# Layer 0 of a two-layer inference step: queries and keys produced with features on partitions, rotated and split there, and passed through DRAM

## The chip, the cores and the metric

The kernel runs on one core of a Trainium2 chip. The metric is the device time of one execution in microseconds (us). The kernel before took 3851.68 us, the median of 3 runs (3841.71 to 3852.99).

## The reference

The reference is one inference step of a two-layer backbone on 128 context tokens (the prompt) and 1024 latent tokens on a grid 64 wide, with a model width of 1024. Layer 0 has two kinds of attention heads side by side, layer 1 retention and RWKV-7; each layer ends in a SwiGLU block. The change is in layer 0's attention:

```python
nq, nk, nv, dq, dk, dv = attn_projections(h_lat, w_in_attn[i])      # also for h_ctx
dq, dk = axial_rope(dq), axial_rope(dk)                              # latent tokens only
o_na = neighbourhood_attention(nq, nk, nv, cache_na_k, cache_na_v, na_rpb)
k_all = concatenate([dk, cache_diff_k]); v_all = concatenate([dv, cache_diff_v])
o_df = diff_attention(dq, k_all, v_all, lam, lam_init)
# axial_rope, on each half of 32 features: x1, x2 = its two quarters
#   concatenate([x1 * cos - x2 * sin, x1 * sin + x2 * cos])
# diff_attention: softmax(q0 k0) - lam * softmax(q1 k1), times v, then an RMS norm
```

There are 4 differential heads (two query and key components of 64 features, values of 128) and 8 neighbourhood heads of 64 features, which attend to a window of 8 grid rows by 16 columns and to 128 cached tokens. The context's keys and values, before any rotation, are outputs too.

## The kernel before, in words

**Numbers in two parts.** Matmuls that must be nearly exact use each fp32 operand as a high part (rounded to the type fp32r) and a low part (the rest). `split` (L71) makes them: ACT copies to the high part (L74), DVE subtracts (L75). A product is then three matmuls, high x high, high x low, low x high.

**The projection.** `attn_in` (L357) makes queries, keys and values for one of eight groups. Groups 0 to 3 are the differential heads, groups 4 to 7 are pairs of neighbourhood heads; each has three blocks of 128 weight columns. `proj_tok` (L332) loads and splits eight weight tiles of 128 x 384 and yields; then for each of 9 tiles of 128 tokens it does 8 x 3 matmuls (L350, L351, L352) whose stationary operand is the normalised input hH or hL and whose moving operand is the weights, 384 columns. The result has tokens on partitions. `sink` copies it from PSUM on ACT (L368), stores it to the DRAM tile qkv on SP's queue (L369), and for the context tile stores keys and values to the outputs. Each group has 10 steps (yields).

**Preparation of keys and queries.** At the start of a head `prep_k` (L409) loads its keys from qkv and the cache in three pieces; `stage` (L380) rotates them where the head is differential (two DVE products, L387 and L394, and a POOL addition, L397), makes the high and low parts (ACT L403 or L405, DVE L406); PE transposes them (L429) and ACT copies them to the tile K (L434, L437), which holds for each component 64 features' high parts on partitions 0 to 63 and the low parts on 64 to 127. Every unit (one query tile of 128 tokens) starts with a load of its queries from qkv (L504, or L615 and L617 for a neighbourhood tile, whose 8 rows of 16 columns are gathered), then `prep_q` (L440) does the same with three slots (high, low, high), four transposes (L446) and a DVE copy (L448) to Q.

**Units and their order.** A differential unit (`diff_unit`, L497) has scores against 9 key tiles (L518, L519), maxima on DVE (L520, L522), exponentials on ACT (L524), the difference of the two softmaxes (L541), transposes of the probabilities (`pv`, L476, with copies at L478) and the products with the values (L482). A neighbourhood unit (`na_unit`, L605) adds its mask and a bias tile nab loaded from DRAM (L624, L649). `pipe` (L567) interleaves the stages of successive units; between every two it calls `fill`, which pulls steps of other work from generators at fixed rates: in the differential stretch the projection of groups 1 to 7 (GS = 0.28 steps a place) and the modulation vectors of `ada_vec` (L165: a load aw on SP's queue and two DVE products, L181; AS = 0.3), in the neighbourhood stretch the output projection (OS = 0.34), its weights (owraw, L744), the transposed input x (L699 to L706) and the mixed tiles (`mix_k`, L750).

**Buffers and queues.** In the pipelined part the accumulator tile "mm" has one buffer; "S" has four, "T" two. Weight tiles have three raw buffers and nine of each part. The instructions are written in the order of the generators, and the compiler's tile framework then orders each engine's queue by a simulated timeline; on the chip every engine, and SP's queue of transfers, works through its own order and waits where an input is missing.

Of the kernel before, what the change touches and what calls it, by code (L numbers as in the profile page):

```python
# [11 lines left out]
F32 = mybir.dt.float32  # L12
F32R = mybir.dt.float32r
I32 = mybir.dt.int32
AF = mybir.ActivationFunctionType
ALU = mybir.AluOpType
# [25 lines left out]
SHARED = ("K", "Q", "pT", "qraw", "kraw", "st2", "st3", "mx", "sm")  # L42


class Net:
# [286 lines left out]
    def proj_tok(self, hH, hL, wsrc, ncol, pool, sink):  # L332

        nc = self.nc
        WH, WL = [], []
        for k in range(KT):
            raw = self.t(pool, [P, ncol], tag="wraw")
            nc.sync.dma_start(raw if ncol != GW else raw.rearrange("p (m c) -> p m c", c=P), wsrc(k))
            wh = self.t(pool, [P, ncol], F32R, tag="wh")
            wl = self.t(pool, [P, ncol], F32R, tag="wl")  # L340
            self.split(wh, wl, raw)
            WH.append(wh)
            WL.append(wl)
        yield
        for T in range(NT):
            pt = self.t(self.nps, [P, 512], tag="mm")
            c = slice(T * P, (T + 1) * P)
            for k in range(KT):
                mm = nc.tensor.matmul
                mm(pt[:, :ncol], lhsT=hH[k][:, c], rhs=WH[k], start=k == 0, stop=False)  # L350
                mm(pt[:, :ncol], lhsT=hH[k][:, c], rhs=WL[k], start=False, stop=False)  # L351
                mm(pt[:, :ncol], lhsT=hL[k][:, c], rhs=WH[k], start=False, stop=k == KT - 1)  # L352
            sink(T, pt)
            yield


    def attn_in(self, g, hH, hL, pool):  # L357
        nc, I, O = self.nc, self.I, self.O
        j = g if g < 4 else g - 4
        blk = 3 if g < 4 else 0  # L360
        w = I["w_in_attn"][0]

        def wsrc(k):
            return w[k * P : (k + 1) * P, :].rearrange("p (m c) -> p m c", c=512)[:, blk : blk + 3, j * P : (j + 1) * P]

        def sink(T, pt):
            st = self.t(pool, [P, GW], tag="ist")
            nc.scalar.copy(st, pt[:, :GW])  # L368
            nc.sync.dma_start(self.qkv[g][T * P : (T + 1) * P, :], st)  # L369
            if T == 0:  # L370
                if g < 4:
                    nc.scalar.dma_start(O[4][0, 0, :, j].rearrange("t c d -> t (c d)"), st[:, P : 2 * P])
                    nc.scalar.dma_start(O[5][0, 0, :, j], st[:, 2 * P :])
                else:
                    nc.scalar.dma_start(O[2][0, 0, :, 2 * j : 2 * j + 2].rearrange("t c d -> t (c d)"), st[:, P : 2 * P])
                    nc.scalar.dma_start(O[3][0, 0, :, 2 * j : 2 * j + 2].rearrange("t c d -> t (c d)"), st[:, 2 * P :])

        return self.proj_tok(hH, hL, wsrc, GW, pool, sink)

    def stage(self, p, raw, n, slots, scale, rope):  # L380

        nc = self.nc
        if rope is not None:
            cs, sn = rope
            m1 = self.t(p, [P, n, P], tag="rm1", bufs=1)
            m2 = self.t(p, [P, n, P], tag="rm2", bufs=1)
            nc.vector.tensor_tensor(  # L387
                m1.rearrange("p n (c d) -> p n c d", d=64),
                raw.rearrange("p n (c d) -> p n c d", d=64),
                cs.unsqueeze(2).to_broadcast([P, n, 2, 64]),  # L390
                op=ALU.mult,
            )
# [8 lines left out]
        if slots == 3:  # L401
            for s in (0, 2):
                nc.scalar.activation(st[:, :, s, :], rv, AF.Copy, scale=scale)  # L403
# [1861 lines left out]
```

## Time and profile before

| What | Value |
|---|---|
| median of 3 runs | 3851.68 us |
| time of the profiled execution | 3851.15 us |
| its span | 3849.4 us |
| PE busy | 3661.5 us (95%) |
| DVE, ACT, POOL busy | 2272.7, 1404.6, 1100.4 us |
| first and last projection matmul of layer 0's attention (L350) | 61.2 and 594.9 us |
| first differential scores, last neighbourhood scores | 126.9 and 878.9 us |

Busy time is the union of an engine's instructions. A line of a stretch's view gives the stretch, its length, and then each engine's busy time with the number of instructions, the mean clock granted to PE, the mean busy share of the 16 DMA engines and GB/s. A line of the groups gives the code line, the engine, what is written from what, the shape and the count; then busy us, mean ns of one, and the idle time of the engine just before them with what ended it. A line of the waits reads: who waited for whom, us in total, times, the longest. The chain of waits is followed back from the end of a stretch, at each step to what released the instruction. SPq is SP's queue of transfers.

### The profile page before, as it was taken

How to read it: one execution, taken by the hardware profiler on the slowest of the kernel's cores; microseconds unless marked ns; L12 is line 12 of the kernel's file. 1: busy time of each engine (PE TensorE's matmuls, PEld its weight loads, DVE VectorE, ACT ScalarE, POOL GpSimd, SP SyncE). 2: the span in 40 equal slices, each digit the busy share in tenths (PEclk: the TensorE clock that was granted, in tenths of full speed). 3: DMA queues.
4: the chain of work that ended last, by engine and by line, in shares of the span. 5: the costliest groups of instructions: out<-in, count | busy, mean ns of one | idle time of the engine just before them, and what ended most of it. 6: DMA issues, size and time to landing. Idle time of an engine off the chain costs nothing.

```text
span 3849.4 us, 67037 instructions
## 1 busy us (share of the span) xinstructions
PE 3661.5 (95%) x24885; PEld 3444.4 (89%) x24885; DVE 2272.7 (59%) x5106; ACT 1404.6 (36%) x3361; POOL 1100.4 (29%) x1450
## 2 busy tenths in 40 slices
PE   7999997999999999999999998999998999999998
PEld 4899996999899999999989886877777899999998
DVE  6677864665945556665244556766665774444434
ACT  3445444555333333225332333233322533334221
POOL 2000002112222224333011323665662322324430
PEclk9999997999999999999999998999999999999999
DMA  6433325542223334442334336232223212223321
GB/s 209 125 94 107 113 69 133 133 109 61 64 85 108 91 99 143 149 137 86 106 105 130 115 129 212 58 88 65 65 60 108 62 60 75 75 73 107 116 88 61
DMA packets 425399, 392.16 MB, mean 102 GB/s; under 512 B 68172, under 2 KB 370376, under 8 KB 423536
## 3 DMA queue, kind: packets, MB, share of 16 engines
q1 hardware_dynamic: 406640, 376.29, 32.3%
q10 hardware_dynamic: 13152, 7.27, 0.7%
q0 software_dynamic: 5280, 4.31, 0.6%
q8 instruction: 197, 3.23, 0.3%
q14 instruction: 130, 1.06, 0.1%
HBM read 289.32 MB, written 98.33 MB: 101 GB/s over the span
## 4 chain that ended last, share of the span: by engine, by line
PE 74%; DVE 8%; DMA 8%; POOL 3%; issue 2%; ACT 2%; SPq 0%; DVEq 0%; ACTq 0%; POOLq 0%
PE mm L82 8%; PE mm L84 8%; PE mm L83 8%; PE A L1726 3%; PE A L1724 3%; PE A L1725 3%; PE o L482 3%; DMA aw<-in_w_ada_dram 2%; PE E L1724 2%; PE E L1725 2%; PE mm L350 2%; PE E L1726 2%; PE mm L352 2%; PE mm L351 2%; DVE aacc L181 2%
## 5 line engine op out<-in xcount | busy, mean ns | idle before, releaser
L729 DVE SCALAR_TENSOR_TENSOR x<-mm,mod,x 128x128 f32<-128x128 f32 (+1 forms) x576 | 277.2, 512 | 238.7 <-PE mm L84 237.9
L1636 POOL TENSOR_TENSOR wl<-raw,wh 128x512 fp32r<-128x512 f32 x120 | 167.1, 1392 | 567.2 <-ACT wh L1635 541.3
L1635 ACT CAST wh<-raw 128x512 fp32r<-128x512 f32 x288 | 178.3, 620 | 306.4 <-PE A L1725 107.4
L181 DVE SCALAR_TENSOR_TENSOR aacc<-aw,v,aacc 128x512 f32<-128x512 f32 x280 | 228.7, 849 | 75.2 <-DMA aw<-in_w_ada_dram 74.7
L350 PE MATMUL mm<-wh,hH 128*128 128x384 f32 x576 | 200.8, 349 | 11.5 <-ACT wh L74 4.7
L352 PE MATMUL mm<-wh,hL 128*128 128x384 f32 x576 | 195.8, 341 | 4.6 <-DVE hL L261 4.6
L351 PE MATMUL mm<-wl,hH 128*128 128x384 f32 x576 | 197.3, 342 | 1.0 <-DVE wl L75 0.9
L82 PE MATMUL mm<-hH,wh 128*128 128x384 f32 x528 | 184.6, 351 | 2.6 <-ACT wh L74 2.6
L84 PE MATMUL mm<-hH,wl 128*128 128x384 f32 x528 | 180.3, 344 | 3.4 <-DVE rst L867 2.1
L83 PE MATMUL mm<-hL,wh 128*128 128x384 f32 x528 | 180.3, 342 | 0.0
L1636 DVE TENSOR_TENSOR wl<-raw,wh 128x512 fp32r<-128x512 f32 x168 | 118.8, 708 | 102.1 <-ACT wh L1635 98.3
L397 POOL TENSOR_TENSOR rm<-rm,rm 128x128 f32<-128x128 f32 (+1 forms) x40 | 27.0, 676 | 461.2 <-DVE rm L387 329.0
L75 DVE TENSOR_TENSOR wl<-wraw,wh 128x256 fp32r<-128x256 f32 (+1 forms) x184 | 90.1, 508 | 108.3 <-ACT wh L74 78.7
L1150 PE MATMUL A<-AR,BK 64*128 64x256 f32 x576 | 116.8, 418 | 31.3 <-DVE KK L1154 18.6
L524 ACT ACTIVATE P<-S,mx 128x384 f32<-128x384 f32 (+1 forms) x200 | 112.2, 570 | 88.8 <-DVE mx L522 86.6
L82 PE MATMUL mm<-mh,owh 128*128 128x384 f32 x384 | 138.5, 375 | 5.2 <-ACT owh L74 2.7
L83 PE MATMUL mm<-ml,owh 128*128 128x384 f32 x384 | 132.5, 345 | 0.0
L84 PE MATMUL mm<-mh,owl 128*128 128x384 f32 x384 | 131.3, 342 | 1.2 <-DVE owl L75 1.2
L350 PEld LDWEIGHTS mm<-wh,hH 128*128 128x128 f32 x576 | 110.2, 191 | 16.2 <-ACT ist L368 7.7
L817 PE MATMUL mm<-wh,hH 128*128 128x256 f32 x432 | 124.0, 290 | 0.0
L1150 PEld LDWEIGHTS A<-AR,BK 64*128 64x128 f32 x576 | 75.4, 194 | 53.1 <-issue 20.0
L818 PE MATMUL mm<-wl,hH 128*128 128x256 f32 x432 | 122.4, 285 | 0.0
(540 smaller groups left out, 12501.5 us busy)
## 6 DMA issues: line engine op xcount, KB each, us to landing
raw<-in_w_ffn_in_dram SPq DMA_DIRECT2D x176, 256.0 KB
aw<-in_w_ada_dram SPq DMA_DIRECT2D x160, 256.0 KB
raw<-hdr SPq DMA_DIRECT2D x132, 192.0 KB
hdr<-c SPq DMA_DIRECT2D x160, 144.0 KB
raw<-in_w_ffn_out_dram SPq DMA_DIRECT2D x88, 256.0 KB
F<-stg SPq DMA_DIRECT2D x34, 640.0 KB
stg<-st SPq DMA_DIRECT2D x12, 1536.0 KB
qkv<-ist SPq DMA_DIRECT2D x72, 192.0 KB
```

The costliest lines, as they stand in the source:

```text
L82: mm(out, lhsT=wh, rhs=xh, start=first, stop=False)
L83: mm(out, lhsT=wh, rhs=xl, start=False, stop=False)
L84: mm(out, lhsT=wl, rhs=xh, start=False, stop=last)
L181: nc.vector.scalar_tensor_tensor(acc[:, c, :], w[:, 0, :], s, acc[:, c, :], op0=ALU.mult, op1=ALU.add)
L350: mm(pt[:, :ncol], lhsT=hH[k][:, c], rhs=WH[k], start=k == 0, stop=False)
L351: mm(pt[:, :ncol], lhsT=hH[k][:, c], rhs=WL[k], start=False, stop=False)
L352: mm(pt[:, :ncol], lhsT=hL[k][:, c], rhs=WH[k], start=False, stop=k == KT - 1)
L729: self.nc.vector.scalar_tensor_tensor(x[f][:, c], pt[:, a:b], self.mod[l][jg][:, f, cd : cd + 1], x[f][:, c], op0=ALU.mult, op1=ALU.add)
L1636: eng.tensor_tensor(wl, w, wh, op=ALU.subtract)
L1724: mm(o, lhsT=wh[:, ks], rhs=xh, start=new and k == 0, stop=False, skip_group_check=True)
L1725: mm(o, lhsT=wh[:, ks], rhs=xl, start=False, stop=False, skip_group_check=True)
L1726: mm(o, lhsT=wl[:, ks], rhs=xh, start=False, stop=k == 3, skip_group_check=True)
```

## The change

The projection's operands change places. Weights are stationary and 384 tokens are moving, so a block comes out as 128 features by 384 tokens, nine (block, token group) tiles a group: keys first, then queries, then values. For the differential heads the weight columns are permuted while they are split (two pieces each), so that the two halves of every rotation pair lie 64 partitions apart; ACT copies the tile and its swapped halves from PSUM, DVE does two products with tables now laid out by feature, and the sum. ACT then writes the high part and DVE, one step later, the low part, and SP stores both to DRAM (qf). For the neighbourhood queries the parts are written in the order of the units' gathered tiles. Values are copied, transposed on PE, copied and stored token by token (vt). The context's output keys are transposed likewise. A head then loads K with two transfers and Q in three pieces of 384 tokens with four transfers each, every row of queries to both halves of the partitions; only the cached keys are split and transposed there (two transposes). These loads run in seven steps, the first six while the head before is in its last three units. The score matmuls use (high, high) and (low, low) queries against K's (high, low). A group has 19 steps, and GS becomes 0.53. The mixed tiles mh and ml have three buffers and a fourth from a later pool.

```diff
+        for m, scale in ((1, None if g < 4 else -0.125), (0, 0.125 if g < 4 else None), (2, None)):
+            ms = slice(m * P, (m + 1) * P)
+            for tg in range(TG):
+                for step in later:
+                    step()
+                later = []
+                sl = slice(tg * GW, (tg + 1) * GW)
+                pt = self.t(self.nps, [P, 512], tag="mm")
+                for k in range(KT):
+                    self.mm3(pt[:, :GW], WH[k][:, ms], WL[k][:, ms], hH[k][:, sl], hL[k][:, sl], k == 0, k == KT - 1)
+                if m == 2:
+                    st = self.t(pool, [P, GW], tag="ist")
+                    nc.scalar.copy(st, pt[:, :GW])
+                    yield
+                    o = turn(st, 3)
+                    dst = self.vt[g][sl, :]
+                    nc.sync.dma_start(dst.rearrange("(n p) c -> p n c", p=P), o.rearrange("p (n c) -> p n c", c=P))
...
+                if g < 4 or m == 1 and tg == 0:
+                    n = GW if g < 4 else P
+                    x = self.t(pool, [P, GW], tag="fx")
+                    nc.scalar.copy(x[:, :n], pt[:, :n])
                 if g < 4:
...
+                    for s in range(2):
+                        nc.scalar.copy(sw[64 * s : 64 * s + 64, a:], pt[64 - 64 * s : 128 - 64 * s, a:GW])
+                    ts = slice(tg * GW + a - P, (tg + 1) * GW - P)
+                    nc.vector.tensor_tensor(sw[:, a:], sw[:, a:], self.sin[:, ts], op=ALU.mult)
+                    nc.vector.tensor_tensor(x[:, a:], x[:, a:], self.cos[:, ts], op=ALU.mult)
+                    nc.vector.tensor_tensor(x[:, a:], x[:, a:], sw[:, a:], op=ALU.add)
+                    yield
+                if m == 1 and tg == 0:
+                    nc.sync.dma_start(ok, turn(x, 1))
+                if g >= 4:
+                    x = pt[:, :GW]
+                for u, v in self.patches(g, m, tg):
+                    nc.scalar.activation(v(hi), u(x), AF.Copy, scale=scale or 1.0)
+                if g >= 4:
+                    yield
+
+                def rest(g=g, m=m, tg=tg, x=x, hl=hl, scale=scale):
+                    hi, lo = hl[:, 0, :], hl[:, 1, :]
+                    for u, v in self.patches(g, m, tg):
+                        if scale is None:
+                            nc.vector.tensor_tensor(v(lo), u(x), v(hi), op=ALU.subtract)
+                        else:
+                            nc.vector.scalar_tensor_tensor(v(lo), u(x), scale, v(hi), op0=ALU.mult, op1=ALU.subtract)
+                    self.store_hl(g, m, tg, hl)
+
+                if g < 4:
+                    later.append(rest)
                 else:
...
+                    rest()
+                yield
...
+    def store_hl(self, g, m, tg, hl):
         nc = self.nc
...
+        dst, a, hl = self.qf[g][m], tg * GW, hl.bitcast(F32)
+        if g < 4:
+            for s in range(2):
+                for i in range(2):
+                    o = dap(dst, (i * P + 32 * s) * TOK + a, [[64 * TOK, 2], [TOK, 32], [1, GW]])
+                    nc.sync.dma_start(o, hl[64 * s : 64 * s + 64, i, :])
+            return
...
+        K = head["K"] = self.t(p, [P, 2, 10 * P], F32R, tag="K")
+        for c in range(2):
+            nc.sync.dma_start(K[:, c, :TOK].bitcast(F32), dap(self.qf[g][1], 64 * c * TOK, [[P * TOK, 2], [TOK, 64], [1, TOK]]))
...
+        def queries(tg):
+            Q = head["Q", tg] = self.t(p, [P, 2, 2, GW], F32R, tag="Q")
+            for c in range(2):
+                for i in range(2):
+                    src = dap(self.qf[g][0], (i * P + 64 * c) * TOK + tg * GW, [[0, 2], [TOK, 64], [1, GW]])
+                    nc.sync.dma_start(Q[:, c, i, :].bitcast(F32), src)
...
+    def heads_hook(self, j, T, heads, gen):
+
+        self.heads_upto(j, 7 if T >= 2 else 6, heads, gen)
+        if T >= 6 and j < 7:
+            self.heads_upto(j + 1, (2, 4, 6)[T - 6], heads, gen)
...
-        GS, AS, OS = 0.28, 0.3, 0.34
+        GS, AS, OS = 0.53, 0.3, 0.34
...
-        bp = _Bufs(both.enter_context(self.pool("kAB")), {"K": 2, "Q": 3, "pT": 2, "qraw": 2, "kraw": 2})
+        bp = _Bufs(both.enter_context(self.pool("kAB")), {"K": 2, "Q": 3, "pT": 2})
...
+            for _ in range(12):
+                next(first)
+            self.heads_upto(0, 5, head, lambda j, h: self.diff_prep(j, h, dp, ps))
+            fin(first)
```

More of the change, by code (lines that the diff above doesn't have):

```diff
@@ L39, in dap @@
     return bass.AP(tensor=ap.tensor, offset=ap.offset + offset, ap=dims)
[L42 removed]
+SHARED = ("K", "Q", "pT", "kraw", "st", "mx", "sm")
 class Net:
@@ new lines, in attn_in @@
+        WH, WL = [], []
+        for k in range(KT):
+            raw = self.t(pool, [P, GW], tag="wraw")
+            src = w[k * P : (k + 1) * P, :].rearrange("p (m c) -> p m c", c=512)[:, blk : blk + 3, j * P : (j + 1) * P]
+            nc.sync.dma_start(raw.rearrange("p (m c) -> p m c", c=P), src)
+            wh = self.t(pool, [P, GW], F32R, tag="wh")
+            wl = self.t(pool, [P, GW], F32R, tag="wl")
+            for a in zip(dense(wh), dense(wl), apart(raw)):
+                self.split(*a)
+            WH.append(wh)
+            WL.append(wl)
@@ L443, in prep_q @@
         pt = self.t(ps, [P, 512], tag="T")
         for c in range(2):
-            for s in range(2):
-                nc.tensor.transpose(pt[:, (c * 2 + s) * P : (c * 2 + s + 1) * P], st[:, c, s * 64 : s * 64 + P], self.ident)
-        Q = self.t(p, [P, 4, P], F32R, tag="Q")
-        nc.vector.tensor_copy(Q.rearrange("p a b -> p (a b)"), pt)
-        return Q
+            nc.tensor.transpose(pt[:, c * P : (c + 1) * P], st[:, c].rearrange("p b c -> p (b c)").bitcast(F32), self.ident)
+        nc.scalar.copy(K[:, :, 9 * P :], pt[:, : 2 * P].rearrange("p (c t) -> p c t", c=2))
@@ new lines, in heads_steps, with heads_upto @@
+        yield
+        queries(1)
+        yield
+        if values is not None:
+            values()
+        yield
+        queries(2)
+        yield
+    def heads_upto(self, j, k, heads, gen):
+        if j not in heads:
+            heads[j] = {"n": 0}
+            heads[j]["gen"] = gen(j, heads[j])
+        while heads[j]["n"] < k:
+            heads[j]["n"] += 1
+            next(heads[j]["gen"], None)
+    def heads_hook(self, j, T, heads, gen):
+        self.heads_upto(j, 7 if T >= 2 else 6, heads, gen)
+        if T >= 6 and j < 7:
+            self.heads_upto(j + 1, (2, 4, 6)[T - 6], heads, gen)
@@ L1943, in run @@
             self.setup(top)
-            self.qkv = [self.dram.tile([TOK, GW], F32, name=f"qkv{g}") for g in range(8)]
+            self.qf = [[self.dram.tile([2, P, TOK], F32, name=f"qf{g}{m}") for m in range(2)] for g in range(8)]
+            self.vt = [self.dram.tile([TOK, P], F32, name=f"vt{g}") for g in range(8)]
             self.odr = [self.dram.tile([TOK, P], F32, name=f"odr{g}") for g in range(8)]
@@ L1979, in attn @@
         wpool = self.wpool
+        done = set()
         def group(g):
-            return self.attn_in(g, hH, hL, wpool)
+            yield from self.first if g == 0 else self.attn_in(g, hH, hL, wpool)
+            done.add(g)
         due = {}
```

278 lines of the change are left out of this document (122 added, 156 removed).

## The prediction

> **What bounds the kernel now.** I read the page's engine totals first, then the busy time by stretch, then the chain of waits inside the stretches that the change touches, then single groups.
>
> ```profile
> PE 3661.5 (95%) x24885; PEld 3444.4 (89%) x24885; DVE 2272.7 (59%) x5106; ACT 1404.6 (36%) x3361; POOL 1100.4 (29%) x1450
> ```
>
> ```profile
> core 0: us, PE busy (x) PEld busy (x) DVE busy (x) ACT busy (x) POOL busy (x), PEclk, DMA share, GB/s
> 60.00:130.00 70.00, 60.49 (x341) 58.59 (x342) 41.40 (x88) 22.11 (x51) 12.21 (x12) 0.95 0.44 127
> 130.00:600.00 470.00, 457.27 (x2965) 445.12 (x2965) 352.07 (x875) 222.49 (x716) 23.39 (x36) 0.99 0.32 96
> 600.00:660.00 60.00, 33.69 (x171) 28.67 (x170) 27.02 (x72) 24.69 (x67) 21.95 (x32) 0.72 0.70 158
> 660.00:890.00 230.00, 222.31 (x1627) 217.17 (x1627) 138.10 (x410) 125.99 (x320) 21.47 (x32) 0.95 0.44 116
> ```
>
> Only 60 to 890 us is touched. The eight projections and the differential heads fill 60 to 600, the neighbourhood heads 640 to 890. PE is busy 457.27 of 470 us in the first long stretch and 222.31 of 230 in the last, so work taken from PE there should shorten the kernel. DVE is next, 352.07 of 470. The stretch 600 to 660 is different: 33.69 us of PE work, a clock of 0.72, and DMA at 0.70. The chain inside 130 to 600 is mostly PE, with a share that PE work does not explain:
>
> ```profile
> by line: PE mm L350 13.8%; PE mm L352 13.5%; PE mm L351 13.5%; PE o L482 9.7%; PE S L518 5.4%; PE S L519 5.2%; DVE aacc L181 5.1%; PE T L476 5.0%; DMA aw<-in_w_ada_dram 4.6%; DMA wraw<-in_w_in_attn_dram 3.5%; issue 2.6%; PE T L446 2.5%; DVE
> ```
>
> The modulation vector (aacc on DVE and its load aw) and the projection weights (wraw) hold 5.1 + 4.6 + 3.5 = 13.2% of it.
>
> **PE: transposes out, fewer transposes in.** The projection's matmul count is unchanged: before, 9 token tiles x 8 x 3 with 384 columns in each group; after, 9 tiles (three blocks, three token groups) x 8 x 3 with 384 tokens. The score matmuls are also the same in number and width. What goes is the transposition of queries (L446) and keys (L429).
>
> ```profile
> L446 PE MATMUL T<-ident,st 128*128 128x128 f32 x288 | 46.8, 288 | 1.7 <-ACT K L437 1.7
> L429 PE MATMUL T<-ident,st 128*128 128x128 f32 x160 | 24.5, 296 | 8.5 <-DVE st L406 8.5
> ```
>
> ```profile
> 304.76 0.60 PE L446 MATMUL T<-ident,st 128*128 128x128 f32 x4
> 305.11 0.42 PE L350 MATMUL mm<-wh,hH 128*128 128x384 f32 x1
> 305.37 0.33 PE L351 MATMUL mm<-wl,hH 128*128 128x384 f32 x1
> 305.54 0.34 PE L352 MATMUL mm<-wh,hL 128*128 128x384 f32 x1
> ```
>
> The 288 ns of one transpose overlap the next; the pace is read from starts. Four transposes begin at 304.76 and the matmul after them at 305.11 (0.35 us), and that matmul takes 0.26 us to its successor where the following one takes 0.17, so a batch of four costs 0.35 + 0.09 = 0.44 us, 0.11 each. Out: 288 + 160 = 448 x 0.11 = 49.3 us. In: the values now come with features on partitions and must be turned back, 9 x 8 = 72 transposes; the context's output keys, 8; the cached keys, 2 x 8 = 16. That is 96 x 0.11 = 10.6 us. Net 38.7 us off PE: half of the removed ones (24.6) lie in the neighbourhood stretch, which gains nearly all of that, while most of the added lie before 600, where 14 to 15 us remain. The other end for this price is the groups' busy time, (46.8 + 24.5)/448 = 0.159 us each, or 56 us net. I take 0.11, because 97% busy PE shows little else between the batches. The filling rate changes with the step count, 252 places x 0.28 for 70 steps to 252 x 0.53 for 133, so projections still end with the last differential unit. The first group's projection keeps its start, set by the normalised input; the larger tables of cosines, the values loaded one step later and the three instead of four buffers of the mixed tiles (the fourth in a late pool) I cost at nothing: their data are used microseconds of PE work after they arrive, and without that cover each would cost one DMA wait, such as the 9.56 or the 10.76 us in the chain below.
>
> The idle time in these two rows, 8.5 + 1.7 = 10.2 us, goes too. Part of it is the start of the neighbourhood stretch:
>
> ```profile
> 623.14 1.92 PE L429 MATMUL T<-ident,st 128*128 128x128 f32 x8 [1.47 <-DVE st L406]
> 626.79 1.12 PE L446 MATMUL T<-ident,st 128*128 128x128 f32 x4 [1.73 <-ACT K L437]
> 631.33 1.97 PE L429 MATMUL T<-ident,st 128*128 128x128 f32 x8 [3.42 <-DVE st L406]
> 634.84 1.12 PE L636 MATMUL S<-K,Q 128*128 128x128 f32 x4 [1.54 <-DVE Q L448]
> ```
>
> ```profile
> 628.74 9.56 DMA kraw<-in_cache_na_k_dram
> ...
> 649.02 10.76 DMA xr<-in_x_sample_dram
> ```
>
> From 623 to 635 PE does nothing but prepare the first neighbourhood head, with 1.47 + 1.73 + 3.42 + 1.54 = 8.2 us of idle. The change loads that head's keys and first queries during the last differential units, so this chain is gone. What is late next is on the same list: the loads of x (10.76 us) behind a DMA share of 0.70, which do not move. I book 5 of the 8.2 us here (bounds 0 and 8.2) and 10.2 - 6.6 = 3.6 us, say 4, elsewhere.
>
> **DVE, ACT, POOL.** The rows are one line of code each by stretch: L448, L406, L387 and L394.
>
> ```profile
> 60.00:600.00 540.00, 24.77 (x36) 0.98 0.34 100
> 600.00:890.00 290.00, 24.73 (x36) 0.90 0.49 125
> ```
>
> ```profile
> 60.00:600.00 540.00, 18.11 (x50) 0.98 0.34 100
> 600.00:890.00 290.00, 16.64 (x46) 0.90 0.49 125
> ```
>
> ```profile
> 60.00:600.00 540.00, 14.78 (x40) 0.98 0.34 100
> ```
>
> ```profile
> 60.00:600.00 540.00, 14.68 (x40) 0.98 0.34 100
> ```
>
> ```profile
> L75 DVE TENSOR_TENSOR wl<-wraw,wh 128x384 fp32r<-128x384 f32 x57 | 32.7, 588 | 13.2 <-ACT wh L74 12.9
> L368 ACT COPY ist<-mm 128x384 f32<-128x384 f32 x72 | 34.6, 481 | 82.1 <-PE mm L352 74.4 <-issue 4.2 <-DMA rpbd<-rpbn 1.3
> L524 ACT ACTIVATE P<-S,mx 128x384 f32<-128x384 f32 (+1 forms) x200 | 112.2, 570 | 88.8 <-DVE mx L522 86.6 <-DMA out_dram<-ist 2.2
> L524 ACT ACTIVATION_READ_ACCUMULATOR P<-S,mx 128x1 f32 x200 | 40.1, 200 | 0.0
> ```
>
> Before 600, DVE loses 24.77 + 18.11 + 14.78 + 14.68 = 72.3 us. It gains three rotations for each of 24 tiles and one subtraction for each of 48, 120 operations of 128x384 at L75's 588 ns = 70.6 us. So DVE stays as it is there, and after 600 it sheds 24.73 + 16.64 = 41.4 us. ACT loses at least L368's 34.6 us and gains some 168 operations at L368's 481 ns (four for each of 24 rotated tiles, one for 24 others, three for the 24 value tiles or their halves taken as two) = 81 us; at most 46 us more on 222.49 of 470 does not bound. POOL loses its additions and gains nothing. Free by cover, then, but through one thing: the projection's accumulator tile "mm" has a single buffer in the pipelined part. It is freed today by one copy. After the change it is read by three ACT copies for rotated tiles, and by ACT and then DVE for the neighbourhood tiles. Today's price of that hold is:
>
> ```profile
> PEld mm L350 <- ACT ist L368: 7.7, 10, 2.0
> PE mm L350 <- ACT ist L368: 4.6, 6, 1.7
> PEld mm L350 <- ACT wh L74: 6.0, 4, 3.5
> PE mm L350 <- ACT wh L74: 4.7, 3, 3.2
> ```
>
> 7.7 + 4.6 = 12.3 us over 72 tiles, 0.17 each. Twice that extra for 24 tiles and once extra for 24: 8.2 + 4.1 = 12.3 us lost. The lower bound is zero, if other work stands between; the upper bound is the slower rival below. Weights of the three later rotated groups are split in two pieces each, and the way from the last projection step of a group to the next group's first is shorter in steps; of the 10.7 us that PE waits for weights I add 3 (0 to 10.7).
>
> **DMA and SP.** The prepared parts go out and come back.
>
> ```profile
> q1 hardware_dynamic: 104432, 83.28, 34.8%
> ```
>
> ```profile
> qkv<-ist SPq DMA_DIRECT2D x72, 192.0 KB
> ```
>
> ```profile
> qraw<-qkv SPq DMA_DIRECT2D x72, 64.0 KB
> kraw<-qkv SPq DMA_DIRECT2D x16, 256.0 KB
> ```
>
> Two thirds of 72 x 192 KB (9.2 MB) of writes become twice that, as high and low parts. Reads of 4.6 + 4.1 MB become 16 key loads of 576 KB and 96 query loads of 192 KB, 27.6 MB, since each query row is loaded twice. That is about 28 MB more. Between 60 and 900 us this queue took 34.8% of 840 us for 83.28 MB, 3.5 us a MB, so 98 us of all engines over 830 us: the share rises by 12 points from 0.32 and 0.44, and stays hidden. On SP, 168 issues (72 stores, 72 + 24 loads) become 292 (148 stores of parts, 24 of values, 8 of output keys, 16 + 96 loads), 124 more; what queues behind a store that waits for its low part are the loads aw and wraw, whose waits are on the chain above. I book nothing for it, and carry it as the third case.
>
> The neighbourhood queries are stored in runs of 128 to 384 bytes, 4096 a group; at this queue's mean, 0.348 x 840 x 16/104432 = 45 ns a packet, four groups take 46 us of all engines. The Trainium skill, DMA: Bandwidth & Descriptors (Specifications), says that below 512 bytes the engine reads, modifies and writes, so these would cost more. If that doubled them, an estimate, it would be 92 us of share, still under the 0.32 that is left to fill; no run so far shows it.
>
> **Sum.** -38.7 - 5 - 4 + 12.3 + 3 = -32.4 us against the profiled execution's own 3851.15: 3818.8, and against the median of 3851.68 shown, half a us more. Forecast 3819.
>
> **The rivals.** Larger gain: the transposes carried their busy price (56 us), the idle goes whole (12 us) and the single buffer costs nothing: 3851 - 68 = 3783. For it: the idle rows above, and 0.72 of clock from 600 to 660. The Trainium skill, TensorE: Matmul & The Clock Gate (Part 1: The HAM clock gate), says idle stretches throttle the array; full clock there would give another 33.69 x 0.28 = 9 us, an estimate. Against it: PE is 97% busy, which leaves little idle to win.
>
> No change: the stretch to 600 is paced by the 13.2% of loads and modulation, now with more traffic on their queue, and passes on nothing; the neighbourhood stretch passes half of its 24. That gives -12 - 9 + 12 + 3 = -6: 3845. Against it: PE's 97%.
>
> Slower: the hold of the one accumulator buffer. Units run from the first row's 126.9 to 606.9 us:
>
> ```profile
> L518 PE MATMUL S<-K,Q x200: 273/338/690, 126.9 to 606.9; 128*128 128x384 f32 x96, 128*128 128x128 f32 x4
> ```
>
> ```profile
> ACT P L524 <- DVE mx L522: 86.6, 45, 5.1
> ```
>
> 480 us/36 = 13.3 us each, seven filling places, so a tile every 2/0.53 x 1.9 = 7.2 us. 24 matmuls at 0.17 take 4.2, which leaves 3.0 us. Three copies take 1.44; three exponentials ahead of them on ACT, (0.57 + 0.20) x 3 = 2.3; and the wait of one of them for DVE's maximum 86.6/45 = 1.9. Together 5.65 us exceeds 3.0 by 2.65, times 24 tiles 64 us, on a sum of -47.7 + 3 without that term: +19, 3870. It decides once the hold passes 3.0 us. The ACT order behind the change decides it, and this trace cannot show that.
>
> **Numbers.** The forecast has 0.50 (its own range 3795 to 3840), the larger gain 0.18, no change 0.15, slower 0.17. Leaving out most of the slower case and the far end of the gain, the range is 3776 to 3856. A measurement of this kernel tells about 0.3%, 11.6 us: faster 0.49 + 0.18 + 0.05 = 0.72, same 0.12, slower 0.16.
>
> **What would show it.** L446's and L429's transposes gone, 96 others in their place; DVE in 130 to 600 near 350 us still; PE's waits for the accumulator's readers near 25 us (over 60 means the slower case); scores of the first neighbourhood head within 3 us of the last differential product; the long stretch shorter by about 10 us, the neighbourhood one by about 20. The forecast is wrong if PE falls clearly under 95% busy before 600.

## The result: 494 us slower, and the profile after

The changed kernel takes 4343.4 us (median of 4 runs, 4338.25 to 4356.9) against 3849.3 us (4 runs) for the kernel before: a ratio of 1.1288, 95% interval [1.1263, 1.1313]. The forecast of 3819 us was wrong in sign. The profiled execution has a span of 4344.8 us, where the kernel before has 3849.4.

The engine totals of the page come first, as they did for the kernel before.

```profile
PE 3737.4 (86%) x24533; PEld 3506.1 (81%) x24533; DVE 2232.2 (51%) x5030; ACT 1395.1 (32%) x3329; POOL 1069.6 (25%) x1410
```

The 352 instructions that should leave PE have left (24885 to 24533), and DVE, ACT and POOL are a little less busy than before. No engine has become the bound; the kernel waits. The busy time by stretch of the changed kernel shows where.

```profile
core 0: us, PE busy (x) PEld busy (x) DVE busy (x) ACT busy (x) POOL busy (x), PEclk, DMA share, GB/s
60.00:130.00 70.00, 42.89 (x201) 40.91 (x201) 37.99 (x78) 17.01 (x38) 9.50 (x8) 0.81 0.22 69
130.00:600.00 470.00, 259.40 (x1385) 243.23 (x1385) 176.54 (x446) 131.67 (x419) 0.00 (x0) 0.75 0.24 79
600.00:940.00 340.00, 267.33 (x1613) 257.63 (x1612) 177.90 (x445) 119.56 (x382) 0.00 (x0) 0.87 0.33 98
940.00:1350.00 410.00, 247.79 (x1445) 239.21 (x1444) 119.56 (x375) 108.88 (x258) 43.15 (x64) 0.71 0.37 106
```

In the 470 us from 130 on PE is busy for 259.40, where it was busy for 457.27, and DVE, ACT and the DMA share (0.24 for 0.32) are all lower than before. When no engine is near full and the mean of the 16 DMA engines is low as well, the limit is one that no mean shows. The score matmuls give the stages' ends (groups on the tile K; the columns after the colon are min/median/max ns, first and last start in us):

```profile
L588 PE MATMUL S<-K,Q x200: 222/346/690, 164.0 to 937.1; 128*128 128x384 f32 x95, 128*128 128x128 f32 x5
L702 PE MATMUL S<-K,Q x16: 220/276/328, 939.7 to 1302.3; 128*128 128x128 f32 x16
L713 PE MATMUL S<-K,Q x128: 220/275/419, 989.8 to 1349.5; 128*128 128x128 f32 x128
```

By these, the first scores are 37 us later (164.0 for 126.9), the differential stretch is 293 us longer (773 for 480), the neighbourhood scores 166 us (410 for 244), and what follows them 25 us; only the gap between the two kinds of head has shrunk, from 28 us to 2.6. Among the longest waits of DVE, ACT and PE for transfers, between 60 and 1330 us of the changed kernel, are these:

```profile
DVE aacc L181 <- DMA aw<-in_w_ada_dram: 94.7, 20, 24.6
ACT ist L364 <- DMA vt<-ist: 83.8, 6, 31.2
ACT wh L74 <- DMA wraw<-in_w_in_attn_dram: 67.0, 21, 14.5
ACT hl L400 <- DMA qf<-hl: 65.0, 14, 27.0
PE S L588 <- DMA Q<-qf: 26.9, 2, 23.8
```

All are transfers of SP's queue: a modulation weight, a store of values that has to leave its buffer, a projection weight, a store of parts, a load of queries. And that queue's own line shows what it is doing (timeline of SP: start, us, line, what, how many):

```profile
121.73 4.62 SPq L471 DMA_DIRECT2D K<-qf  x2
126.39 22.33 SPq L448 DMA_DIRECT2D qf<-hl  x4
148.77 31.04 SPq L481 DMA_DIRECT2D Q<-qf  x8
179.91 10.65 SPq L448 DMA_DIRECT2D qf<-hl  x4
190.60 3.38 SPq L384 DMA_DIRECT2D vt<-ist  x2
```

In these 72 us SP issues 20 transfers. Eight query loads of 192 KB hold it for 31.04 us: 1.57 MB in 31.04 us is 51 GB/s. The stretch in the middle of these loads, where nearly nothing else moves, is this:

```profile
155.00:175.00 20.00, 3.32 (x8) 1.93 (x8) 0.45 (x2) 0.46 (x2) 0.00 (x0) 0.50 0.13 50
```

A share of 0.13 of 16 engines is 2.1 engines, and in the trace's packets exactly two are under way in 87% of these 20 us, never more than three. The transfers run on two DMA engines, while PE works 3.32 of 20 us. In the diff three kinds of transfer have a 2 as the first, slowest dimension of their DRAM side: the differential stores `[[64*TOK, 2], [TOK, 32], [1, GW]]`, the key loads `[[P*TOK, 2], [TOK, 64], [1, TOK]]` and the query loads `[[0, 2], [TOK, 64], [1, GW]]`. That is 96 x 96 KB, 16 x 576 KB and 96 x 192 KB, together 37.7 MB, which at 51 GB/s keep a pair of engines busy for 740 us.

The Trainium skill, DMA: Bandwidth & Descriptors (Why a DMA increments its semaphore by 16 and not by 1), states it: a transfer goes to the largest number of engines, at most 16, that divides the slowest dimension (other than 1) of each of its two access patterns. For these three kinds that is 2, and the share of 0.13 agrees. The prediction overlooked this rule.

So theory A is that the shape of these three patterns makes the loss, and its first rival is that the 28 MB of added traffic do, whatever its shape. Other rivals were the short runs of the neighbourhood queries' stores, the hold of the one accumulator buffer, and the order of loads behind stores.

### The profile page after: what moved, and what is told of

It reads as the page before. It is cut to its first block, busy times and chain, and to the rows that moved or that the text cites. A ratio compares the mean times of both kernels' runs of the same rounds, so it can differ in the third digit from the quotient of the medians.

```text
span 4344.8 us, 66247 instructions
## 1 busy us (share of the span) xinstructions
PE 3737.4 (86%) x24533; PEld 3506.1 (81%) x24533; DVE 2232.2 (51%) x5030; ACT 1395.1 (32%) x3329; POOL 1069.6 (25%) x1410
## 2 busy tenths in 40 slices
DMA packets 445331, 420.67 MB, mean 97 GB/s; under 512 B 82732, under 2 KB 388008, under 8 KB 443472
## 4 chain that ended last, share of the span: by engine, by line
PE 60%; DMA 11%; DVE 6%; POOL 3%; issue 2%; ACT 1%; SPq 1%; DVEq 0%; ACTq 0%; POOLq 0%
PE mm L82 8%; PE mm L84 8%; PE mm L83 8%; PE A L1792 3%; PE A L1790 3%; PE A L1791 3%; DMA aw<-in_w_ada_dram 2%; PE E L1790 2%; PE E L1791 2%; PE E L1792 2%; PE o L554 2%; DMA F<-stg 1%; DMA owraw<-in_w_out_attn_dram 1%; DMA xr<-odr 1%; PE mm L883 1%
## 5 line engine op out<-in xcount | busy, mean ns | idle before, releaser
L82 PE MATMUL mm<-hH,wh 128*128 128x384 f32 x1104 | 399.4, 363 | 88.4 <-ACT hl L400 46.9
L83 PE MATMUL mm<-hL,wh 128*128 128x384 f32 x1104 | 388.1, 352 | 8.8 <-DVE hL L261 8.8
L84 PE MATMUL mm<-hH,wl 128*128 128x384 f32 x1104 | 387.4, 352 | 3.2 <-DVE rst L933 2.4
L82 PEld LDWEIGHTS mm<-hH,wh 128*128 128x128 f32 x1104 | 220.2, 200 | 105.5 <-ACT hl L400 50.8
L83 PEld LDWEIGHTS mm<-hL,wh 128*128 128x128 f32 x1104 | 219.9, 199 | 12.3 <-DVE hL L261 9.4
L84 PEld LDWEIGHTS mm<-hH,wl 128*128 128x128 f32 x1104 | 218.6, 198 | 8.2 <-issue 2.9
L75 DVE TENSOR_TENSOR wl<-wraw,wh 128x256 fp32r<-128x256 f32 (+2 forms) x216 | 91.4, 447 | 198.1 <-ACT wh L74 169.2
L554 PE MATMUL o<-V,pT 128*128 128x128 f32 x584 | 90.1, 299 | 60.5 <-DVE mx L592 33.9
L590 DVE TENSOR_REDUCE mx<-S 128x1 f32<-128x384 f32 (+1 forms) x200 | 101.5, 540 | 68.3 <-PE S L589 68.1
L554 PEld LDWEIGHTS o<-V,pT 128*128 128x128 f32 x584 | 84.2, 211 | 64.1 <-ACT pT L550 27.1
```

Source lines behind the costliest of these rows:

```text
L82: mm(out, lhsT=wh, rhs=xh, start=first, stop=False)
L83: mm(out, lhsT=wh, rhs=xl, start=False, stop=False)
L84: mm(out, lhsT=wl, rhs=xh, start=False, stop=last)
L554: nc.tensor.matmul(o, lhsT=pT[:, i * P : (i + 1) * P], rhs=vs(b + i), start=b + i == 0, stop=b + i == nk - 1)
```

## The experiments

**wide_all** keeps number, bytes and contents of the transfers and puts the dimension of 32 or 64 rows first.

```diff
-                for i in range(2):
-                    o = dap(dst, (i * P + 32 * s) * TOK + a, [[64 * TOK, 2], [TOK, 32], [1, GW]])
-                    nc.sync.dma_start(o, hl[64 * s : 64 * s + 64, i, :])
+                for c in range(2):
+                    o = dap(dst, (64 * c + 32 * s) * TOK + a, [[TOK, 32], [P * TOK, 2], [1, GW]])
+                    nc.sync.dma_start(o, hl[64 * s + 32 * c : 64 * s + 32 * c + 32, :, :])
...
-        for c in range(2):
-            nc.sync.dma_start(K[:, c, :TOK].bitcast(F32), dap(self.qf[g][1], 64 * c * TOK, [[P * TOK, 2], [TOK, 64], [1, TOK]]))
+        for i in range(2):
+            nc.sync.dma_start(K[64 * i : 64 * i + 64, :, :TOK].bitcast(F32), dap(self.qf[g][1], i * P * TOK, [[TOK, 64], [64 * TOK, 2], [1, TOK]]))
...
-                for i in range(2):
-                    src = dap(self.qf[g][0], (i * P + 64 * c) * TOK + tg * GW, [[0, 2], [TOK, 64], [1, GW]])
-                    nc.sync.dma_start(Q[:, c, i, :].bitcast(F32), src)
+                for d in range(2):
+                    src = dap(self.qf[g][0], 64 * c * TOK + tg * GW, [[TOK, 64], [P * TOK, 2], [1, GW]])
+                    nc.sync.dma_start(Q[64 * d : 64 * d + 64, c, :, :].bitcast(F32), src)
```

> All three new kinds of transfer (stores of parts for the differential heads, key loads, query loads) are cut the other way: the dimension of 32 or 64 rows comes first and the dimension of 2 behind it. Number of transfers, bytes and runs of 1536 or 4608 bytes are the same. Theory A (a transfer whose first dimension is 2 is carried by two of the 16 DMA engines, and those two are the bound; eight query loads of 192 KB took 31 us in the changed kernel, 51 GB/s, and 37.7 MB go that way, 744 us): the loss goes, 3790 to 3870 us. Theory B (the single accumulator buffer is held too long by its three readers): nothing changes, 4330 to 4360. Theory C (the way through DRAM and SP's queue with its 124 more issues is the cost, whatever their shape): nothing changes, 4330 to 4360.

Measured: 3893.14 us (4 runs), 1.0102 [1.0064, 1.0139] of the kernel before. Of the 494 us, 450 are gone by the shape alone. The time is 23 us above the range of theory A; theories B and C, by which nothing changes, are out as the cause of the loss. The issues of query loads (L481) and of modulation weights (L128) on SP, first in the changed kernel and then in wide_all (min/median/max ns):

```profile
L481 SPq DMA_DIRECT2D Q<-qf x96: 486/1446/5928, 148.8 to 1301.4; - x96
L128 SPq DMA_DIRECT2D aw<-in_w_ada_dram x59: 327/340/12132, 62.8 to 867.7; - x59
```

```profile
L481 SPq DMA_DIRECT2D Q<-qf x96: 573/602/1252, 112.4 to 859.0; - x96
L128 SPq DMA_DIRECT2D aw<-in_w_ada_dram x59: 327/334/1640, 63.8 to 566.4; - x59
```

The median query load occupied SP for 1446 ns and now takes 602; and a weight load, whose own pattern was not touched, could take 12132 ns and now takes 1640 at most. The two-engine transfers held up everything behind them on the queue. The stretches of wide_all show PE back at work, with a DMA share that is twice the changed kernel's 0.24:

```profile
126.00:640.00 514.00, 475.94 (x2955) 457.18 (x2955) 350.43 (x883) 248.56 (x789) 0.00 (x0) 0.97 0.50 132
640.00:910.00 270.00, 223.64 (x1457) 216.64 (x1458) 119.34 (x372) 108.86 (x257) 43.15 (x64) 0.84 0.68 158
```

**wide_q** and **wide_k_st** recut only the query loads, and only the key loads and stores.

> Only the query loads are cut the other way; key loads and stores keep a first dimension of 2. Theory A: 18.9 of 37.7 MB are left on the pair, 372 us of its time, spread over some 800 us and partly hidden: 3850 to 4050 us. Theories B and C: 4330 to 4360.

> The mirror image: key loads and stores are cut the other way, query loads keep a first dimension of 2. Theory A: again 18.9 MB are left on the pair, so about the same as with only the query loads recut, 3850 to 4050 us; the sum of the two gains is larger than the whole loss if the pair is a bound that saturates. Theories B and C: 4330 to 4360.

Measured: 4097.87 us, 1.063 [1.0608, 1.0652], and 4139.63 us, 1.0739 [1.0711, 1.0767] (2 runs each). The query loads' shape is worth 245 us and that of the other two 204, together 449 where both at once give 450. Each half is 18.9 MB, so 11 to 13 us a MB. Both times lie above the range of theory A, 3850 to 4050: less of the pair's time was hidden than it supposed. The expectation held it possible that the two gains together would exceed the whole; they do not.

**old_traffic** and **old_narrow** give the kernel before (without the change) the added traffic: each tile of the projection is stored a second time, and each unit copies a tile of 192 KB within DRAM, 28 MB more in all. They differ in the DRAM patterns alone: 128 rows in the first, 2 x 64 rows in the second.

```diff
             nc.sync.dma_start(self.qkv[g][T * P : (T + 1) * P, :], st)
+            nc.sync.dma_start(self.qkv2[g][T * P : (T + 1) * P, :GW], st)
...
             nc.sync.dma_start(raw[:, 0, :], self.qkv[j][T * P : (T + 1) * P, 0:P])
+            nc.sync.dma_start(self.qkv2[j][T * P : (T + 1) * P, GW:], self.qkv2[j][T * P : (T + 1) * P, :GW])
```

In old_narrow the added lines are these:

```diff
+            nc.sync.dma_start(dap(self.qkv2[g], T * 64 * 2 * GW, [[HT * 2 * GW, 2], [2 * GW, 64], [1, GW]]), st)
...
+            two = [[HT * 2 * GW, 2], [2 * GW, 64], [1, GW]]
+            nc.sync.dma_start(dap(self.qkv2[j], T * 64 * 2 * GW + GW, two), dap(self.qkv2[j], T * 64 * 2 * GW, two))
```

> The kernel before, with about the traffic that the change adds and nothing of its work: every projection tile is stored a second time (72 x 192 KB), and every unit copies one such tile from DRAM to DRAM (72 x 192 KB) that nobody reads; 28 MB, in rows of 1536 bytes with a first dimension of 128. Theory A2 (traffic on all 16 engines delays the loads that set the pace): 3865 to 3890. If the traffic stays hidden, as the forecast had it: 3848 to 3858.

> The kernel before with the same 28 MB of extra traffic as in the earlier run on it (72 stores and 72 DRAM copies of 192 KB, read by nobody), but the DRAM side of each is cut 2 x 64 rows instead of 128 rows, the halves in two places. Theory A (a first dimension of 2 puts a transfer on two of the 16 engines): 28.3 MB at 51 GB/s are 555 us of the pair, in a stretch of 830 us; at the 11 to 13 us a MB that the two half recut kernels showed, 300 to 370 us slower, and at least 100 if much of it hides since nobody reads the data. If the loss was due to something else in the changed kernel that the recut changed too: 3860 to 3866, as with the wide rows.

Measured: 3862.6 us, 1.0032 [1.0019, 1.0044], and 4223.12 us, 1.096 [1.0923, 1.0996]. The same bytes cost 12 us in one shape, between the two ranges that were expected, and 372 in the other, where theory A had 300 to 370. The stretch 130 to 600 in old_traffic, then in old_narrow:

```profile
130.00:600.00 470.00, 451.92 (x2890) 438.82 (x2889) 347.58 (x863) 218.09 (x701) 24.30 (x37) 0.97 0.47 144
```

```profile
130.00:600.00 470.00, 295.65 (x1637) 282.98 (x1638) 195.41 (x474) 124.23 (x391) 16.11 (x22) 0.78 0.29 92
```

The second line has the look of the changed kernel: PE at 295.65 of 470, a clock of 0.78, and a DMA share that is lower, not higher, than in the first. In the packets of this stretch exactly two are under way in 48% of the time, in old_traffic in 2%. Theory A holds in both directions, and the rival of the mere traffic is left with some 12 us.

**old_twice** measures the price of the transposes: in the kernel before, each unit's four query transposes are done twice, 288 more.

```diff
-        for c in range(2):
+        for c in (0, 1, 0, 1):
             for s in range(2):
                 nc.tensor.transpose(pt[:, (c * 2 + s) * P : (c * 2 + s + 1) * P], st[:, c, s * 64 : s * 64 + P], self.ident)
```

> The kernel before, with the four transposes of every unit's queries done twice into the same place: 288 more transposes, nothing else. If a transpose on PE costs its 0.11 us on the path, as the forecast had it: 32 us more, 3875 to 3890. If PE has room for them (the forecast's gain was never there to be had): 3848 to 3860.

Measured: 3863.99 us, 1.004 [1.0023, 1.0058]. 1.004 is 15 us (9 to 22) over 288, 0.053 us each, half of the 0.11 that the prediction read from starts. The time lies between the two ranges. In the profiled execution the work from the first differential to the last neighbourhood scores is 19 us longer (771.2 for 752.0), which agrees. If a removed transpose is worth what an added one costs, the 352 net transposes that the change removes are worth 19 us, an estimate, not 38.7.

The remaining runs ask why wide_all, with fewer transposes, is still 1% slower than the kernel before.

**pool_dup**: wide_all with each query load done once, and GpSimd copying it to the other 64 partitions.

```diff
-                for d in range(2):
...
-                    nc.sync.dma_start(Q[64 * d : 64 * d + 64, c, :, :].bitcast(F32), src)
+                nc.sync.dma_start(Q[0:64, c, :, :].bitcast(F32), src)
+                nc.gpsimd.tensor_copy(Q[64:P, c, :, :], Q[0:64, c, :, :])
```

> On the kernel with all transfers recut (3893 us): each query piece is loaded once, to partitions 0 to 63, and GpSimd, which is idle in this stretch, copies it to partitions 64 to 127. 48 query transfers fewer, 9.4 MB less, 48 GpSimd copies of 64x768 more. Theory A2 (what is left of the loss is the larger traffic: the DMA share of 0.5 before 600 us and 0.8 after 650): 3855 to 3880. Theory B2 (what is left is the hold of the single accumulator buffer and the ACT and DVE order behind it): 3885 to 3900. Theory D (the rest is the first group, whose feature tiles wait for the whole normalised input): 3885 to 3900.

Measured: 3864.84 us (9 runs), 1.0047 [1.0033, 1.0061]. By the ratios, about half of wide_all's excess came from loading each query twice, in traffic and in 48 issues together, as theory A2 had it.

**first_tg**: wide_all with group 0's token groups in the order 1, 2, 0 and the first head's loads one step later, to let its first loads stand ahead.

```diff
-            for tg in range(TG):
+            for tg in (1, 2, 0) if g == 0 else range(TG):
...
-            for _ in range(12):
+            for _ in range(13):
```

> On the kernel with all transfers recut (3893 us): only for the first group the three token groups are taken in the order 1, 2, 0 (and the key loads start one step later), because the input's first token group is normalised last; the first group took 63.8 to 122.3 us where it took 61.2 to 108.6 before. Theory D: 3875 to 3885. Theories A2 and B2: 3885 to 3900.

Measured: 3884.44 us, 1.0086 [1.0067, 1.0106], inside wide_all's interval and on the border of the two ranges: no gain that can be told.

**turns**: wide_all with the accumulator taken from the tags mm, S and T in turn through the differential stretch, so that no tile waits for the readers of the one before.

```diff
             fin(first)
-            self.nps = ps
```

> On the kernel with all transfers recut (3893 us): the projection's accumulator takes the tags mm, S and T in turn for the whole differential stretch instead of the single buffer mm. Theory B2: the waits of PE for the accumulator's readers go, 3865 to 3885, unless scores and transposes lack the buffers. Theories A2 and D: 3885 to 3900.

Measured: 3930.51 us, 1.0201 [1.0181, 1.0221], slower than wide_all by 37 us and outside both ranges. The projection's tiles then come out of the buffers of the scores and the transposes: in the differential stretch PE's waits for the accumulator's readers fall from some 11 us to some 2, but the scores wait 20.8 us for ACT's exponentials where wide_all has 4.5. So this run alone does not price the hold.

**plainq**: wide_all with the neighbourhood queries' parts stored in token order, whole rows instead of runs of 128 to 384 bytes. It leaves out their reordering for the units' gathered tiles.

```diff
-        if g < 4 or m == 1:
+        if True:
...
-        if m == 1:
+        if True:
             nc.sync.dma_start(dap(dst, a, [[TOK, P], [P * TOK, 2], [1, GW]]), hl)
```

> On the kernel with all transfers recut (3893 us): the neighbourhood queries are written and stored in token order like the keys, one transfer a tile instead of two to four, no run under 1536 bytes; the reordering of the queries for the units' gathered tiles is left out, all else is done. If the 16,384 runs of 128 to 384 bytes cost something (a part of theory A2): 3870 to 3885. Theories B2 and D: 3885 to 3900.

Measured: 3877.41 us, 1.0071 [1.0051, 1.0091], about 12 us less than wide_all by the ratios, with intervals that overlap, so not clear of the noise.

**pool_first** joins wide_all, pool_dup and first_tg; **pool_plain_first** adds plainq's edit.

> All transfers recut, queries loaded once and copied by GpSimd, first group in the order 1, 2, 0: the sum of the two gains, 3865 - 8 = 3857 us if they add up; 3865 if the first group's order is worth nothing.

> The same with the neighbourhood queries written and stored in token order, so that their reordering is left out: 3857 - 16 = 3841 us if the three gains add up, which would be just under the kernel before; 3857 if the short runs cost only where the traffic is high.

Measured: 3866.91 us, 1.0035 [1.0017, 1.0053], and 3865.89 us, 1.0034 [1.0019, 1.0049]. The gains do not add up: the first group's order is worth nothing that can be told on top of pool_dup, and pool_plain_first is 9 us above the higher of its two values. With the queries loaded once, the short runs cost nothing that can be told.

**pool_swap**: pool_first with the swapped halves copied by GpSimd from SBUF, so that one ACT copy frees the accumulator of a differential tile.

```diff
-                        nc.scalar.copy(sw[64 * s : 64 * s + 64, a:], pt[64 - 64 * s : 128 - 64 * s, a:GW])
+                        nc.gpsimd.tensor_copy(sw[64 * s : 64 * s + 64, a:], x[64 - 64 * s : 128 - 64 * s, a:GW])
```

> The best of the recut kernels so far (queries loaded once, first group in the order 1, 2, 0; ratio 1.0035), with the two swapped halves of a rotated tile copied by GpSimd from the copy in SBUF instead of by ACT from the accumulator: the accumulator is free after one ACT copy instead of three, and ACT has 48 copies less before 600 us. If the hold of the accumulator and ACT's queue are what is left of the loss (theory B2), the ratio falls by 0.002 to 0.004, to about that of the kernel before. If not, it stays at 1.003 to 1.005.

Measured: 3867.24 us, 1.0035 [1.0017, 1.0053], the same as pool_first. In its differential stretch PE's waits for the accumulator's readers fall from some 12 us to some 5, while the waits of the scores for ACT's exponentials rise from 4.0 us to 9.5. Freeing the accumulator earlier gives nothing of the rest back.

**no_dep** and **no_store**, both on pool_first: every head loads group 0's keys and queries, so that no load waits for a recent store; and, in the second, groups 1 to 7 do not store their parts either.

```diff
-            nc.sync.dma_start(K[64 * i : 64 * i + 64, :, :TOK].bitcast(F32), dap(self.qf[g][1], i * P * TOK, [[TOK, 64], [64 * TOK, 2], [1, TOK]]))
+            nc.sync.dma_start(K[64 * i : 64 * i + 64, :, :TOK].bitcast(F32), dap(self.qf[0][1], i * P * TOK, [[TOK, 64], [64 * TOK, 2], [1, TOK]]))
...
-                src = dap(self.qf[g][0], 64 * c * TOK + tg * GW, [[TOK, 64], [P * TOK, 2], [1, GW]])
+                src = dap(self.qf[0][0], 64 * c * TOK + tg * GW, [[TOK, 64], [P * TOK, 2], [1, GW]])
```

In no_store also:

```diff
-                    self.store_hl(g, m, tg, hl)
+                    if g == 0:
+                        self.store_hl(g, m, tg, hl)
```

> All transfers recut, queries loaded once, first group in the order 1, 2, 0 (ratio 1.0035); all heads load the keys and queries of group 0, so that no load waits for a store of its own group; those of the other groups are stored and not used. Leaves out the use of seven groups' queries and keys. If the way out and back through DRAM (loads that wait for stores, with SP's queue behind them) is what is left: ratio 0.993 to 1.000. If not: 1.002 to 1.005.

> The same, and groups 1 to 7 do not store their parts at all (16.5 MB and some 120 transfers less): work left out. If the rest of the loss is the stores' traffic and SP's time for them: ratio 0.993 to 0.999, near the forecast's 0.992. If it is in the engines' order (ACT, DVE and PE waits of the new projection): 1.000 to 1.004.

Measured: 3874.42 us, 1.0057 [1.0037, 1.0076], and 3875.57 us, 1.0079 [1.0054, 1.0104]: both are a little above their upper ranges, neither is faster than pool_first, and why no_store is slower is not shown. Its long stretch has the DMA share of the kernel before, 0.32, and PE is still idle for 29.5 of 495 us, as in pool_dup (28.7):

```profile
130.00:625.00 495.00, 465.49 (x2882) 449.47 (x2883) 345.43 (x857) 238.67 (x755) 26.22 (x28) 0.96 0.32 86
```

So neither the wait of loads for stores nor the stores themselves are what is left. One reservation holds for all these small differences: an edit also changes the order in which the framework puts each engine's queue, and these runs do not separate the two.

## Why the prediction was wrong, step by step

**The step that failed** is the paragraph on DMA and SP: "98 us of all engines over 830 us: the share rises by 12 points from 0.32 and 0.44, and stays hidden", and "I book nothing for it". The bytes were right (392.16 MB before, 420.67 after, by the pages), but the price of a byte was taken from transfers that use 16 engines and given to patterns that use two. 37.7 MB then take 740 us of the same pair, not a few points of everything. The share of 0.32 "left to fill" was the wrong test: it fell to 0.24 while the kernel lost 494 us. The prediction did see who stands behind on SP's queue (aw and wraw, and aw leads the waits above), but thought of the wait for a low part and not of the transfer itself. Its own test, that it is wrong if PE falls clearly under 95% busy before 600, is the line that showed it: 259.40 of 470 us.

**PE.** The count was right: 448 out, 96 in, 352 less on the page. The price was not: 0.053 us each by old_twice, so by that estimate a term of 19 us where the sum has 38.7. PE was 97% busy before, and yet 288 more transposes added half of what their pace says; why is not shown. The range that the prediction gave for this price, 0.11 to 0.159, did not reach low enough.

**The neighbourhood stretch.** Its start was right. The first neighbourhood scores were to come within 3 us of the last differential product; they come before it (939.7 and 949.6 us in the changed kernel, 628.9 and 635.3 in pool_dup), 2.6 and 3.8 us after the last differential scores, where it was 28 before. But the prediction also gave this stretch nearly all of its half of the transposes, 24.6 us, because PE was 222.31 of 230 us busy there. That part failed. The rows of the gathered tiles' scores, before and in pool_dup, and the stretches between their first and last starts:

```profile
L645 PE MATMUL S<-K,Q x128: 337/344/669, 640.8 to 878.6; 128*128 128x384 f32 x128
L711 PE MATMUL S<-K,Q x128: 337/343/525, 645.4 to 884.0; 128*128 128x384 f32 x128
```

```profile
640.80:878.60 237.80, 224.62 (x1611) 218.81 (x1610) 140.51 (x416) 127.69 (x330) 32.21 (x48) 0.93 0.49 126
645.40:884.00 238.60, 208.58 (x1377) 204.55 (x1376) 111.64 (x348) 101.42 (x236) 57.42 (x82) 0.86 0.65 149
```

PE has 16 us less to do and the stretch is no shorter. The idle time on PE grows from 13 to 30 us, and the largest waits in pool_dup's stretch are these:

```profile
PE S L709 <- DVE mx L715: 12.4, 6, 6.5
PE T L771 <- DMA xr<-in_x_sample_dram: 7.9, 3, 4.6
```

```profile
DVE sb L715 <- DMA nab<-rpbd: 20.6, 7, 4.9
```

Before, the three were 2.3, 3.6 and 6.8 us. PE waits for the masked maxima on DVE, and DVE for the bias tiles nab, which hold 12.5% of this stretch's chain of waits where they held 4.5%. Loads stand behind the largest waits there, at a DMA share of 0.65 for 0.49, and the clock is lower too, 0.86 for 0.93. At the start of the stretch the prediction had named the loads that do not move as "late next", and there they take back part of the gain: the gathered tiles' first scores come 20 us after the last differential ones, 34 before, at a DMA share of 0.86 (pool_dup).

```profile
625.00:690.00 65.00, 41.33 (x222) 36.96 (x221) 25.99 (x78) 25.59 (x66) 23.85 (x33) 0.71 0.86 200
```

**DVE, ACT, POOL.** Right, as far as the recut kernels show: DVE was to stay near 350 us in the long stretch and takes 346.64 us of pool_dup's 495, against 352.07 of 470 before; ACT rises, 240.45 for 222.49, and bounds nothing.

```profile
130.00:625.00 495.00, 466.29 (x2911) 450.91 (x2909) 346.64 (x861) 240.45 (x762) 22.57 (x24) 0.97 0.46 121
```

**The accumulator, the weights and what is left.** The forecast added 12.3 us for the hold and 3 for the weights. The differential stretch by its own scores, before (126 to 608) and in pool_dup (121 to 626), and the largest waits of PE there:

```profile
126.00:608.00 482.00, 465.83 (x3022) 452.58 (x3020) 361.35 (x899) 228.31 (x736) 23.99 (x37) 0.99 0.32 96
```

```profile
121.00:626.00 505.00, 472.80 (x2941) 455.87 (x2940) 351.80 (x877) 245.09 (x778) 24.16 (x26) 0.97 0.47 123
```

```profile
PE mm L350 <- ACT wh L74: 4.1, 2, 3.2
...
PE mm L350 <- ACT ist L368: 2.9, 5, 1.3
```

```profile
PE mm L82 <- ACT wh L74: 7.8, 4, 5.0
PE T L361 <- ACT ist L380: 4.5, 3, 3.1
...
PE mm L82 <- DVE hl L419: 3.9, 3, 3.1
PE mm L82 <- ACT hl L400: 2.7, 6, 0.9
```

With 81 fewer PE instructions the stretch between the first and last scores is 23 us longer; the prediction had it some 10 us shorter. 16 us of the 23 are more idle time on PE (32.2 for 16.2), of which these rows name 3.7 for weights, 4.5 for the new transposes of values and 3.7 for the accumulator's readers; 7 us are more busy time, at a clock of 0.97 for 0.99. The term for the weights, 3 us, is of the size of its row. The term for the hold, 12.3 us, is about three times its rows, and the slower rival (64 us of hold) did not come. The hold was sized on 7.7 + 4.6 us, which adds the wait of a weight load to the wait of its own matmul: in the trace of before the two end at the same moments (116.74 and 116.75, 242.03 and 242.03), so PE itself lost 4.6 us, and the prediction's own rule would then have given 4.6 and not 12.3.

Yet pool_swap, which frees the accumulator earlier, gave no time back, and no_dep and no_store, which take other waits away, are no faster than pool_first. pool_first is 16 us above the kernel before by the medians (7 to 20 by the interval) where the forecast, on its own terms but without the price of shape, has 32 below. The transposes' price would account for some 20 of these 48 us, and old_traffic's 12 us may stand for part of the 19 MB that pool_dup still moves more (411.25 for 392.16 MB); but no_store, with less traffic, was not faster. By stretch, in pool_dup, most of the shortfall is the differential one, 23 us longer instead of 10 shorter; from its last scores to the last neighbourhood scores the kernel gains 13 us instead of about 20. What makes up the rest in the differential stretch stays open; the order of the engines' work in the new projection is a guess that no run shows. No version that was tried beats the kernel before.

**The rivals.** The larger gain did not come, for the transposes are worth less and not more. The slower rival had the right sign by the wrong mechanism (its 24 x 0.17 is 4.1 and not 4.2, which moves its 64 us by less than 3). No change, "now with more traffic on their queue", had the right place, without the price. The short runs, which the Trainium skill, DMA: Bandwidth & Descriptors (Specifications), led the prediction to weigh at up to 92 us of share, cost nothing that can be told in pool_first against pool_plain_first. In the changed kernel's trace packets of 128, 256, 384 and 512 bytes took 13, 18, 22 and 27 ns in the median, so the runs take some 20 us of all engines, not 46 or 92: no run here shows a clear penalty under 512 bytes.

## What to carry to other kernels

Before a transfer is priced by its bytes, read the first dimension of both of its access patterns: where it was 2 here, the bytes went through two engines, at some 50 GB/s, with everything else on that queue behind them. Putting the long dimension first, with the same bytes and the same number of transfers, gave back 450 us here. A low mean DMA share beside idle compute engines does not say that transfers are free; look at how long the queue's own issues last. Price a removed instruction on a busy engine by doubling it in the old kernel, not by its pace. And ask what takes over once the engine has less to do: in the neighbourhood stretch 16 us less work on PE left the time as it was, while its waits for loads grew.

## What the hardware showed that was not expected

- Two engines: a DMA share of 0.13 and 50 GB/s over 20 us in which eight transfers of 192 KB with a first dimension of 2 were under way; 28 MB more in this shape cost 372 us, and 12 us with a first dimension of 128.
- The issue itself is held up: a query load's issue on SP lasted 1.4 us in the median and 5.9 at most, and one weight load's 12.1 us behind such transfers; after the recut 0.60 and 1.6.
- The starved PE was also granted less clock, 0.75 from 130 to 600 us where it had 0.99, and 0.50 in the 20 us of the row above.
- 288 more transposes of 128x128 on a PE that is 97% busy cost 15 us, 0.053 each, though four in a row, read from starts, take 0.11 each.
